# Half a gated block and VectorE's key tiles ahead of the key-value product and the sample updates; a new layout for the adaLN product

## The chip, the cores and the metric

The kernel runs on one core of a Trainium2 chip. Five engines work side by side, each with its own fixed list of instructions: TensorE (PE in the profile; its weight loads are PEld), VectorE (DVE), ScalarE (ACT), GpSimd (POOL) and SyncE (SP), whose queue here issues nearly all transfers. They wait for each other by semaphores. The metric is device time of one execution in microseconds; lower is better. The kernel before was timed in three runs: 1280.69, 1283.85 and 1285.78 us, median 1283.85.

## The reference, cut to what matters

One inference step of a trunk of two layers, for 512 prompt tokens and 8 sample tokens (520 in all), width 1024, four heads of 256. Each layer mixes an mLSTM branch and a causal convolution branch:

```python
mod = jax.nn.silu(c) @ w_ada + b_ada
shift, scale, gate = jnp.split(mod[:, None, :], 3, axis=-1)
h = rmsnorm(x, norm_w) * (1.0 + scale) + shift
proj = h @ w_in
xm, zm, ga, gb, zc, gm, gc = jnp.split(proj, N_SPLITS, axis=-1)
...
h, C, n, m = mlstm_chunkwise(q, k, v, i_pre, logf, C0, n0, m0)
hm = (hm + skip * xm_c) * jax.nn.silu(zm)
y_m = hm @ w_br_m
u = ga * jax.nn.sigmoid(gb)
u, cbuf = causal_dwconv(u, cbuf0, cconv_w, cconv_b)
u = jax.nn.silu(layernorm(u, cln_w, cln_b))
u = u * jax.nn.silu(zc)
y_c = u @ w_br_c
merged = jax.nn.sigmoid(gm) * y_m + jax.nn.sigmoid(gc) * y_c
x = x + gate * (merged @ w_out)
```

The chunkwise mLSTM amounts to this for the prompt: weights from gates and scores, `S = (q k^T) * exp(D)`; numerator `S v`; and a new memory `C = sum ws k v^T`, which is an output. For each sample token the old memory `C0` is scaled and a rank-one term is added: `C_new = a * C + ws * k v^T`, an output too.

## The kernel before, in words

**Dense products.** `dense` (L180) multiplies a 128-column weight with all tokens in two halves of 260, in three products of split numbers (high by high, high by low, low by high): 24 matmuls of 128x260 a half, 48 for an output block. `split_w` (L163) loads a raw weight on SP's queue, ACT casts it to the high part (whi, L173), POOL subtracts for the low part (wlo, L176).

**Order.** A scheduler orders the instructions of each engine before the run. It follows the program's order as priority, its own estimate of times, and `tc.issue_after(ins)`, which lets the instructions in its block be placed only behind `ins`. PSUM comes from pools: three buffers with tag "d" (dense products), three with tag "m", two with tag "cv".

**adaLN.** The modulation has six chunks of 512 columns a layer. Chunks 0 to 3 hold scale and shift; hh and hl, the high and low part of the normed input, need one for each two k. Chunks 4 and 5 hold the gate, which only `residual` (L321) reads, at the end of the layer. `ada_load` brings a chunk in four loads of 512 KB. `ada_mul` (L286) multiplies it: 8 matmuls of 32x512, one for each k, into the column group k % 4, so that the group sums stand in four sets of 32 rows; ACT copies 128x512 (asb, from the pool "t520" of four buffers). Its `tail` sums the four groups and turns them with four matmuls with a selection matrix (sel32), and VectorE adds the bias into mod. In the first layer chunks 0 to 3 run inside the first gated block (`dense_pair`, L237, the rows L248), whose k-th step needs the k-th hh. Chunks 4 and 5 follow that block. The second layer's chunks 0 and 1 are multiplied in the first layer's GM and GC stages, the others at the layer's change and just behind it.

**Stages of a layer.** gab 0 (first gated block of the convolution branch), xm with q, k, v, the gates, gab 2, then the heads (L924 to L941), normaliser and output of the mLSTM, ZM, GM (merge gate of the mLSTM, L1013 to L1026), GC, layer norm, ZC, BRC, OUT.

**Heads.** For head h: `values` turns v (ptok) and splits it into v1h and v1l; `scores` makes pu and pds and the weights dd and P; `sample` loads the memories of two sample tokens (cb) and multiplies them with q (pqc); `nxt`, the first part of a gated block left over from the head before; `apply` multiplies P with v (ppv); `keys` turns k (ptok) and scales it into a high part on ACT (kwh) and a low part on VectorE (kw); `updates` change cb (POOL scales, L777, and VectorE adds, L780) and write it out; `gab_b` (L527) runs the second part of the next gated block, 48 dense matmuls; `memory` is the key-value product (pcf) from kwh, kw and v. Before the first head, pst and pvt turn the gates and the samples' values.

Of the kernel before, what the change touches and what calls it, by code (L numbers as in the profile page):

```python
# [1 line left out]

# [1 line left out]

# [16 lines left out]
L = 2  # L21
# [8 lines left out]
H = 4  # L30
# [45 lines left out]
def build(nc, tc, ctx, ap):  # L76
# [60 lines left out]
    class Pairs:  # L137
# [7 lines left out]
        def tail(self, i, n):  # L145
            return self.tiles[i][:, :, T - n:T]

    def t520(name):
        return tmp.tile([128, T], F32, tag="t520", bufs=T5B, name=name)
# [127 lines left out]
    def ada_load(l, c, tag):  # L277
        raw = ada_tile(tag)
        for kp in range(0, 4, 2):
            ada_half(l, c, raw, kp)  # L280
        return raw

    def ada_chunk(l, adas, c, tag, ps=("m", 3)):
        return ada_mul(adas, c, ada_load(l, c, tag), ps)

    def ada_mul(adas, c, raw, ps=("m", 3), stream=False):  # L286
        vec, mod, sa = adas
        acc = pm("ada", *ps)
        for n in range(KT):
            k = n if stream else KT - 1 - n  # L290
            r = 32 * (k % 4)
            te.matmul(acc[r:r + 32, :], cT[:, k, :], raw[k // 2][:, k % 2, :], start=(n < 4), stop=(n >= 4))  # L292
        asb = t520("asb")
        s.copy(asb[:, 0:512], acc)

        def tail():
            pt = pm("adat", *ps)
            ks = slice(c * 4, c * 4 + 4)
            for i in range(4):
                te.matmul(pt[:, i * 9:i * 9 + 9], asb[:, i * 128:(i + 1) * 128], sel32[:, 0:9], start=True, stop=True)  # L300
            v.tensor_tensor(out=mod[:, ks, :], in0=pt[:, 0:36].rearrange("p (m r) -> p m r", r=9),
                            in1=vec[:, O_BADA + c * 4:O_BADA + c * 4 + 4].unsqueeze(2).to_broadcast([128, 4, 9]),
                            op=ALU.add)
            if c < 4:
                o = 2 * c
                v.scalar_tensor_tensor(out=sa[:, o:o + 2, :], in0=mod[:, 4 * c:4 * c + 2, :], scalar=1.0,
                                       in1=vec[:, O_NORM + o:O_NORM + o + 2].unsqueeze(2).to_broadcast([128, 2, 9]),
                                       op0=ALU.add, op1=ALU.mult)
        return tail
# [100 lines left out]
    for l in range(L):  # L410
# [113 lines left out]

            return [first, second] + [lambda sft=sft: tap(1 - sft % 2, sft) for sft in range(3, W31)] + [last]

        def gab_b(k, raw=False, w=None):  # L527
            wb, wa = w or split_w(ap["wst"][l, PR_GAB + k], 2)
            sg = t520("sg")

            def evb(c, p):
                if raw or w:
                    s.copy(sg[:, c], p)
                    if w and c is HALF[1]:
                        s.activation(sg, sg, AF.Sigmoid)
                else:
                    s.activation(sg[:, c], p, AF.Sigmoid)

            def eva(c, p):
                v.tensor_tensor(out=u[:, k, c], in0=p, in1=sg[:, c], op=ALU.mult)  # L540

            def gab_a():
                if w:
                    dense_pair(wb, wa, hh, hl, evb, eva, hook)
                    mm = None
                else:
                    mm = dense(wa, hh, hl, KT, eva)
                nc.sync.dma_start(ap["o_conv_p"][l, :, k], u[:, k, TP - W31 + 1:TP])
                conv31_sample(k)
                filler.extend(conv31_tasks(k))  # L550
                return mm

            if not w:
                dense(wb, hh, hl, KT, evb)
                if raw:
                    s.activation(sg, sg, AF.Sigmoid)
            return gab_a

        def gab(k, raw=False, w=None):
            return gab_b(k, raw, w)()  # L560

        mtail = sml.tile([128, KT, W4 - 1], F32, tag="mtail", name="mtail")

# [58 lines left out]
            return proj(tuple(a[:, 512:1024] for a in w), xcs, kk, h, DH ** -0.5)  # L622

        gab(0, w=w01)
        if l == 0:
            gtails = [ada_chunk(l, adas, 4, "q"), ada_chunk(l, adas, 5, "v")]
        else:
            gtails.append(ada_mul(adas, *raws.pop(0)))
        for tail in gtails:
            tail()  # L630
        xc = big.tile([128, KT, T], F32, tag="xc", name="xc")
        q = big.tile([128, KT, T], F32, tag="q", name="q")
        kk = Pairs("k", F32, "kk")
# [123 lines left out]
        def sample(b):  # L757
            cb = s8.tile([128, KT, V1], F32, tag="s8", bufs=S8B, name="cb")
            nc.sync.dma_start(cb, ap["C0"][l, b])
            vb = s8.tile([128, H, V1], F32, tag="s4", bufs=2, name="vb")  # L760
            nc.sync.dma_start(vb.rearrange("p h c -> p (h c)"),
                              vsc[b].rearrange("h c -> (h c)").partition_broadcast(128))
            p = pm("pqc")
            for j in range(2):
                for h in range(H):
                    k = 2 * h + j
                    o = (k * TS + b) * TS
                    te.matmul(p[32 * h:32 * h + 32, 0:V1], zq[:, o:o + 32], cb[:, k, :],  # L768
                              start=(j == 0), stop=(j == 1))
            if b == 0:  # L770
                v.tensor_copy(qc, p[:, 0:V1])
            else:
                v.tensor_tensor(out=qc, in0=qc, in1=p[:, 0:V1], op=ALU.add)

            def update():
                for h in range(H):
                    g.tensor_scalar(out=cb[:, 2 * h:2 * h + 2, :], in0=cb[:, 2 * h:2 * h + 2, :],  # L777
                                    scalar1=bc[:, 0, h, b:b + 1], scalar2=1.0, op0=ALU.mult, op1=ALU.mult)
                    for j in range(2):
                        v.scalar_tensor_tensor(out=cb[:, 2 * h + j, :], in0=vb[:, h, :], scalar=wsk[:, h, j, b:b + 1],  # L780
                                               in1=cb[:, 2 * h + j, :], op0=ALU.mult, op1=ALU.add)
                nc.sync.dma_start(ap["o_C_s"][l, b], cb)

            return update

# [33 lines left out]
        def tok_major(src, h, a):  # L819
            p = pm("ptok")  # L820
            for b in range(2):
                for j in range(2):
                    o = (b * 2 + j) * 128
                    t0 = (2 * a + b) * 128
                    te.transpose(p[:, o:o + 128], src[:, 2 * h + j, t0:t0 + 128], ident)  # L825
            return p

        def mul3(p, first, last, ah, al, bh, bl):
# [3 lines left out]
        def mlstm(h):  # L832
# [42 lines left out]
            def keys():  # L875
                st["kwl"] = []
                p = [tok_major(kk, h, a) for a in range(2)]
                kwh = big.tile([128, 4, DH], F32R, tag=f"k{h}", name="kwh")
                st["kwh"] = kwh
                for a in range(2):  # L880
                    kt = tmp.tile([128, 2, DH], F32R, tag="t520", bufs=T5B, name="kw")
                    for b in range(2):
                        i = 2 * a + b
                        pb = p[a][:, b * 256:(b + 1) * 256]
                        s.activation(kwh[:, i, :], pb, AF.Copy, scale=ws[:, i:i + 1])
                        v.scalar_tensor_tensor(out=kt[:, b, :], in0=pb, scalar=ws[:, i:i + 1],
                                               in1=kwh[:, i, :].bitcast(F32), op0=ALU.mult, op1=ALU.subtract)
                        st["kwl"].append(kt[:, b, :])

            def apply():  # L890
                Ph, Pl = st["P"]
# [33 lines left out]
        for h in range(H):  # L925
            values, scores, keys, apply, memory = mlstm(h)
            values()
            pl = scores()
            if h == 0:
                sample_factors()  # L930
            updates = [sample(2 * h + i) for i in range(2)]
            if nxt:
                nxt()
            apply()
            keys()
            with tc.issue_after(pl.ins):
                updates[0]()
            nxt = gab_b(h + 3, True)
            memory()
            updates[1]()  # L940
            fill(F_H)  # L941

        s1 = sml.tile([128, 1], F32, name="s1")
# [64 lines left out]

        mrg = Pairs("v", F32, "mrg")
        if l + 1 < L:  # L1010
            adas = ada_start(l + 1)
            raw = ada_load(l + 1, 0, "xc")
        for m in range(KT):  # L1013
            wg, wb = split_w(ap["wst"][l, PR_GMB + m], 2)
            sg = t520("sgm")
            dense(wg, hh, hl, KT, lambda c, p: s.activation(sg[:, c], p, AF.Sigmoid))

            def ev(c, p):
                i = v.tensor_tensor(out=mrg[:, m, c], in0=p, in1=sg[:, c], op=ALU.mult)
                with tc.issue_after(i.ins):  # L1020
                    fill(F_GM)

            mm = dense(wb, hmh, hml, KT, ev)
            if l + 1 < L and m == 3:
                with tc.issue_after(mm.ins):
                    tail = ada_mul(adas, 0, raw)  # L1026

        sgc = Pairs("k", F32, "sgc")
        if l + 1 < L:
# [171 lines left out]
```

## Time and profile before

| | before |
|---|---|
| median of three runs | 1283.85 us |
| the profiled execution | 1279.5 us |
| its span, first to last instruction | 1277.8 us |
| mean granted TensorE clock | 0.993 |
| VectorE busy | 843.3 us (66%) |
| ACT busy | 531.8 us (42%) |
| POOL busy | 682.4 us (53%) |

The profile is of one execution. Its span leaves out 1.7 us of its own time. All rows below are of that execution and count from the start of the span. A row of a timeline gives start, duration, engine, line, operation, output and input tiles, shape, count of records, and in brackets how long the engine was idle before it and what ended that. A group's row gives busy time, mean duration of one in ns, and idle time before. One fp32 matmul leaves two records; a matmul of split numbers leaves one.

### The profile page before, as it was taken

The page shows a single profiled execution, that of the slowest core. Times are in us where ns is not written, and L with a number is a line of the kernel's source. Part 1 is how long each engine was busy: PE and PEld are TensorE (multiplying, and loading weights), DVE is VectorE, ACT ScalarE, POOL GpSimd, SP SyncE. Part 2 cuts the span into 40 slices and gives each one's busy share as a digit, 9 for nine tenths or more (in the row PEclk, how much of TensorE's full clock was granted, in tenths as well). Part 3 has the DMA queues.
Part 4 walks back from the last instruction along what each step waited for, and adds up shares of the span by engine and source line. Part 5 has one row for each costly group of instructions (what it writes and reads, how often), then busy time and mean ns, then how long its engine had stood idle before and what let it go on. Part 6 is the DMA issues. An engine that isn't in the chain of part 4 may idle for free.

```text
span 1277.8 us, 25802 instructions
## 1 busy us (share of the span) xinstructions
PE 1226.5 (96%) x10244; PEld 1155.6 (90%) x10244; DVE 843.3 (66%) x1735; ACT 531.8 (42%) x955; POOL 682.4 (53%) x899
## 2 busy tenths in 40 slices
PE   6999999999999999999999999999999999999996
PEld 3699988889999999899979997888899999989996
DVE  6495576667977993544257748666788899735424
ACT  3466554443332223532236655445434222344342
POOL 2356545556654446565635664444485545467572
PEclk9999999999999999999999999999999999999998
DMA  9632346653342342243932324566422232223322
GB/s 361 232 95 78 115 159 246 218 183 124 100 166 83 99 149 84 75 149 108 336 136 85 101 82 137 205 211 241 164 88 97 86 99 85 84 83 123 127 83 67
DMA packets 59929, 177.14 MB, mean 139 GB/s; under 512 B 13409, under 2 KB 21665, under 8 KB 55713
## 3 DMA queue, kind: packets, MB, share of 16 engines
q1 hardware_dynamic: 56928, 167.08, 38.6%
q10 hardware_dynamic: 2880, 8.42, 1.8%
q8 instruction: 80, 1.31, 0.4%
q14 instruction: 41, 0.33, 0.1%
HBM read 149.77 MB, written 25.71 MB: 137 GB/s over the span
## 4 chain that ended last, share of the span: by engine, by line
PE 80%; DVE 10%; ACT 3%; DMA 3%; POOL 2%; issue 1%; SPq 1%; DVEq 0%; ACTq 0%; POOLq 0%
PE pd L188 66%; DVE cb L780 4%; PE pds L864 3%; PE pd L248 2%; DMA o_C_p<-cf 2%; POOL wlo L176 2%; PE ada L292 1%; ACT whi L173 1%; PE pqc L768 1%; PE pcf L830 1%; DVE cv L515 1%; PE ppv L830 1%; PE pg L664 1%; DMA wada<-w_ada 1%; PE ptok L825 1%
## 5 line engine op out<-in xcount | busy, mean ns | idle before, releaser
L176 POOL TENSOR_TENSOR wlo<-raw,whi 128x256 fp32r<-128x256 f32 x680 | 523.5, 802 | 523.5 <-ACT whi L173 518.8
L188 PE MATMUL pd<-hh,whi 128*128 128x260 f32 x1728 | 495.4, 287 | 6.9 <-ACT szc L1051 5.3
L188 PE MATMUL pd<-hl,whi 128*128 128x260 f32 x1728 | 491.2, 284 | 0.0
L188 PE MATMUL pd<-hh,wlo 128*128 128x260 f32 x1728 | 490.8, 284 | 0.0
L188 PEld LDWEIGHTS pd<-hh,whi 128*128 128x128 f32 x1728 | 326.6, 189 | 14.5 <-ACT szc L1051 5.8
L188 PEld LDWEIGHTS pd<-hl,whi 128*128 128x128 f32 x1728 | 327.0, 189 | 0.4 <-issue 0.2
L188 PEld LDWEIGHTS pd<-hh,wlo 128*128 128x128 f32 x1728 | 326.8, 189 | 0.3 <-POOL wlo L176 0.2
L173 ACT CAST whi<-raw 128x1024 fp32r<-128x1024 f32 (+1 forms) x174 | 179.1, 1030 | 329.8 <-PE pd L188 276.4
L515 DVE SCALAR_TENSOR_TENSOR cv<-u,vec,cv 128x509 f32<-128x509 f32 (+6 forms) x448 | 296.5, 729 | 0.1
L780 DVE SCALAR_TENSOR_TENSOR cb<-vb,wsk,cb 128x257 f32<-128x257 f32 x128 | 72.7, 616 | 4.0 <-POOL cb L777 4.0
L188 PE MATMUL pd<-hmh,whi 128*128 128x260 f32 x256 | 72.4, 283 | 0.0
L188 PE MATMUL pd<-hml,whi 128*128 128x260 f32 x256 | 72.4, 283 | 0.0
L188 PE MATMUL pd<-hmh,wlo 128*128 128x260 f32 x256 | 72.3, 283 | 0.0
L188 PE MATMUL pd<-zl,whi 128*128 128x260 f32 x256 | 72.0, 283 | 0.0
L188 PE MATMUL pd<-zh,wlo 128*128 128x260 f32 x256 | 72.0, 283 | 0.0
L188 PE MATMUL pd<-zh,whi 128*128 128x260 f32 x256 | 71.8, 283 | 0.0
L188 PE MATMUL pd<-ml,whi 128*128 128x260 f32 x224 | 63.3, 283 | 0.0
L188 PE MATMUL pd<-mh,whi 128*128 128x260 f32 x224 | 63.3, 283 | 0.0
L188 PE MATMUL pd<-mh,wlo 128*128 128x260 f32 x224 | 63.2, 283 | 0.0
L324 DVE SCALAR_TENSOR_TENSOR xr<-pd,mod,xo 128x260 f32<-128x260 f32 (+1 forms) x32 | 15.3, 484 | 61.7 <-PE pd L188 38.9
L777 POOL TENSOR_SCALAR cb<-cb,bc 128x514 f32<-128x514 f32 x64 | 51.5, 825 | 1.3 <-PE pqc L768 1.3
L188 PE MATMUL pd<-xcs,whi 128*128 128x260 f32 x256 | 47.9, 287 | 3.0 <-ACT vv L568 2.9
(306 smaller groups left out, 2251.3 us busy)
## 6 DMA issues: line engine op xcount, KB each, us to landing
raw<-wst SPq DMA_DIRECT2D x160, 512.0 KB, 3.8
wada<-w_ada SPq DMA_DIRECT2D x36, 512.0 KB, 8.1
cb<-C SPq DMA_DIRECT2D x16, 1028.0 KB, 6.5
o_C_s<-cb SPq DMA_DIRECT2D x16, 1028.0 KB, 5.4
vb<-vsc SPq DMA_DIRECT2D x16, 514.0 KB, 5.5
wada<-w_ada ACTq DMA_DIRECT2D x12, 512.0 KB, 5.8
raw<-wqkv SPq DMA_DIRECT2D x8, 512.0 KB, 3.5
x<-x SPq DMA_DIRECT2D x4, 520.0 KB, 7.0
```

What stands on the lines that cost most here:

```text
L173: s.copy(hi, sl)
L176: g.tensor_tensor(out=lo[:, cs], in0=sl[:, cs], in1=hi.bitcast(F32)[:, cs], op=ALU.subtract)
L188: mm = te.matmul(p[:, 0:HT], a[:, ws], b[:, k, HALF[c]], start=(n == 0), stop=(n == 3 * nk - 1))
L248: te.matmul(p[:, 0:HT], a[:, ws], b[:, k, HALF[c]], start=(k == 0 and i == 0), stop=(k == KT - 1 and i == 2))
L292: te.matmul(acc[r:r + 32, :], cT[:, k, :], raw[k // 2][:, k % 2, :], start=(n < 4), stop=(n >= 4))
L324: v.scalar_tensor_tensor(out=x[:, m, c.start:c.start + n], in0=p[:, 0:n], scalar=mod[:, 16 + m, 0:1], in1=xo[:, c.start:c.start + n], op0= ...
L515: v.scalar_tensor_tensor(out=acc[a][:, sft:TP], in0=u[:, k, 0:TP - sft], scalar=wcol(sft), in1=acc[a][:, sft:TP], op0=ALU.mult, op1=ALU.add)
L664: te.matmul(pgs[n][32 * j:32 * j + 32, 0:HT], vec[:, o:o + 32], (q, kk, vv)[t][:, k, c], start=(r == 0), stop=(r == 5))
L777: g.tensor_scalar(out=cb[:, 2 * h:2 * h + 2, :], in0=cb[:, 2 * h:2 * h + 2, :], scalar1=bc[:, 0, h, b:b + 1], scalar2=1.0, op0=ALU.mult, o ...
L780: v.scalar_tensor_tensor(out=cb[:, 2 * h + j, :], in0=vb[:, h, :], scalar=wsk[:, h, j, b:b + 1], in1=cb[:, 2 * h + j, :], op0=ALU.mult, op ...
L830: te.matmul(p, a, b, start=(first and n == 0), stop=(last and n == 2))
L864: te.matmul(p[:, 0:n], kk[:, 2 * h + j, t0:t0 + 128], q[:, 2 * h + j, t0:TP], start=(j == 0), stop=(j == 1))
```

## The change

It has three parts.

1. **Layout of the adaLN product.** `ada_mul` makes 32 matmuls of 32x128 for a chunk instead of 8 of 32x512: for each k, four, one for each 128 columns, each into a column group of its own. The result is then already summed over k, 128x128. ACT copies 128x128 into a buffer of its own (tag "asb", two buffers) and no longer into "t520". The tail is one transpose instead of four matmuls.
2. **Place of chunks 4 and 5 of the first layer.** They leave their place behind gab 0 and come in the first layer's GM stage, behind m = 1 and m = 3, with their tails; the second layer's chunk 0 moves from m = 3 to m = 5. All three are loaded into the tile "xc", one after the other.
3. **Heads.** `gab_b` runs its first half as before and its second half behind the last transpose of kk; `memory` may be placed only behind the last matmul of that second half. The updates of the first of the two sample tokens are cut in two: heads 0 and 1 behind the scores, heads 2 and 3 behind the last kw too. Those of the second come behind the last kw. In the program `keys` now stands behind the first of these.

```diff
         for n in range(KT):
             k = n if stream else KT - 1 - n
-            r = 32 * (k % 4)
-            te.matmul(acc[r:r + 32, :], cT[:, k, :], raw[k // 2][:, k % 2, :], start=(n < 4), stop=(n >= 4))
-        asb = t520("asb")
-        s.copy(asb[:, 0:512], acc)
+            for j in range(4):
+                mm = te.matmul(acc[32 * j:32 * j + 32, 0:128], cT[:, k, :],
+                               raw[k // 2][:, k % 2, j * 128:(j + 1) * 128], start=(n == 0), stop=(n == KT - 1))
+        asb = sml.tile([128, 128], F32, tag="asb", bufs=2, name="asb")
+        s.copy(asb, acc[:, 0:128])
...
-            for i in range(4):
-                te.matmul(pt[:, i * 9:i * 9 + 9], asb[:, i * 128:(i + 1) * 128], sel32[:, 0:9], start=True, stop=True)
+            te.transpose(pt[:, 0:128], asb, ident)
...
-                dense(wb, hh, hl, KT, evb)
+                dense(wb, hh, hl, KT, evb, (0,))
+                with tc.issue_after(behind.ins) if behind else nullcontext():
+                    mm = dense(wb, hh, hl, KT, evb, (1,))
...
-        if l == 0:
-            gtails = [ada_chunk(l, adas, 4, "q"), ada_chunk(l, adas, 5, "v")]
-        else:
+        if l:
             gtails.append(ada_mul(adas, *raws.pop(0)))
...
             apply()
-            keys()
             with tc.issue_after(pl.ins):
-                updates[0]()
-            nxt = gab_b(h + 3, True)
-            memory()
-            updates[1]()
+                updates[0](range(2))
+            turned, kw = keys()
+            with tc.issue_after(kw.ins), tc.issue_after(pl.ins):
+                updates[0](range(2, H))
+            nxt, mm = gab_b(h + 3, True, behind=turned)
+            with tc.issue_after(mm.ins):
+                memory()
+            with tc.issue_after(kw.ins):
+                updates[1](range(H))
...
         if l + 1 < L:
+            late = adas
             adas = ada_start(l + 1)
-            raw = ada_load(l + 1, 0, "xc")
+            turns = [(late, l, 4), (late, l, 5), (adas, l + 1, 0)]
+            raw = ada_load(*turns[0][1:], "xc")
...
             mm = dense(wb, hmh, hml, KT, ev)
-            if l + 1 < L and m == 3:
+            if l + 1 < L and m % 2 == 1 and turns:
+                who, _, c = turns.pop(0)
                 with tc.issue_after(mm.ins):
-                    tail = ada_mul(adas, 0, raw)
+                    tail = ada_mul(who, c, raw)
+                if turns:
+                    raw = ada_load(*turns[0][1:], "xc")
+                    tail()
```

The engines' lists show where this puts the work. At three places they stand as follows; a row gives the line, the operation, output and input tiles, the shape, and how often it stands there in a row.

PE, first head of the first layer, before: pst and pvt turn gates and samples, ptok turns v, the pd rows are dense matmuls, pu begins the scores.

```order
L188 MATMUL pd<-hh,whi 128x260
L710 MATMUL pst<-ident,sxt 128x128 x4
L719 MATMUL pvt<-ident,vv 32x128 x8
L825 MATMUL ptok<-ident,vv 128x128 x2
L727 MATMUL pvt<-ones,prod 32x2 x8
L825 MATMUL ptok<-ident,vv 128x128 x2
L188 MATMUL pd<-hl,whi 128x260
```

The same place of the changed kernel:

```order
L188 MATMUL pd<-hh,wlo 128x260
L711 MATMUL pst<-ident,sxt 128x128 x4
L720 MATMUL pvt<-ident,vv 32x128 x8
L827 MATMUL ptok<-ident,vv 128x128 x4
L728 MATMUL pvt<-ones,prod 32x2 x8
L827 MATMUL ptok<-ident,vv 128x128 x4
L862 MATMUL pu<-ur,selr 128x512
L864 MATMUL pu<-mneg,identr 128x128
L866 MATMUL pds<-q,kk 128x512 x2
```

Before, the last row shown is the first of 20 dense matmuls; then come ptok, one more dense matmul, pu, and 17 more ahead of pds: 38. Now none stands between pst and pds, and 99 instead of 109 stand ahead of pst since the gates' work. The 48 come later, 25 of them between the transposes of kk and the first pcf.

VectorE, first head of the first layer, from the samples' product on, before: cb are the updates, bst and mv the statistics of the head's output, kw the key tiles, u the gated block's evacuation.

```order
L780 SCALAR_TENSOR_TENSOR cb<-vb,wsk,cb 128x257 x4
L798 BN_AGGR mv<-bst 128x2
L780 SCALAR_TENSOR_TENSOR cb<-vb,wsk,cb 128x257 x2
L800 SCALAR_TENSOR_TENSOR dn<-q,en 128x4
L797 BN_STATS bst<-q 128x6
L780 SCALAR_TENSOR_TENSOR cb<-vb,wsk,cb 128x257 x2
L886 SCALAR_TENSOR_TENSOR kw<-ptok,wsl,kwh 128x256 x2
L797 BN_STATS bst<-q 128x6
L540 TENSOR_TENSOR u<-pd,sg 128x260
```

The changed kernel there:

```order
L802 SCALAR_TENSOR_TENSOR dn<-q,en 128x4
L800 BN_AGGR mv<-bst 128x2
L803 TENSOR_TENSOR dn<-dn,q 128x4
L889 SCALAR_TENSOR_TENSOR kw<-ptok,wsl,kwh 128x256 x4
L781 SCALAR_TENSOR_TENSOR cb<-vb,wsk,cb 128x257 x12
L841 MEMSET v1l 128x4x2
L851 MEMSET v1h 128x4x2
L540 TENSOR_TENSOR u<-pd,sg 128x260
L850 TENSOR_TENSOR v1l<-ptok,v1h 128x2x256 x2
```

Four of the sixteen updates stay ahead of the statistics; the four kw come next, and the other twelve updates stand in one row behind them, ahead of u and v1l.

PE at the start, the end of gab 0's k loop, before: ada is the adaLN product, adat its tail, the L248 rows are gab 0.

```order
L292 MATMUL ada<-wada,cT 32x512 x2
L300 MATMUL adat<-sel_83,asb 128x9 x4
L248 MATMUL pd<-hh,whi 128x260 x2
L292 MATMUL ada<-wada,cT 32x512
L248 MATMUL pd<-hl,whi 128x260
```

The changed kernel's last chunk there, whose next rows are gab 0's last third with dense matmuls of xm (L188) between:

```order
L248 MATMUL pd<-hh,wlo 128x260
L300 MATMUL adat<-ident,asb 128x128
L188 MATMUL pd<-hh,whi 128x260
L188 MATMUL pd<-hl,whi 128x260
L248 MATMUL pd<-hh,whi 128x260 x2
L188 MATMUL pd<-hh,wlo 128x260
L188 MATMUL pd<-hh,whi 128x260
```

Before, gab 0 had chunk 4's product between its last rows (the single ada row and seven more behind it). Now twenty dense matmuls of xm stand there.

More of the change, by code (lines that the diff above doesn't have):

```diff
@@ L1 @@
-from contextlib import ExitStack
+from contextlib import ExitStack, nullcontext
 import numpy as np
@@ L298, in tail @@
             ks = slice(c * 4, c * 4 + 4)
-            for i in range(4):
-                te.matmul(pt[:, i * 9:i * 9 + 9], asb[:, i * 128:(i + 1) * 128], sel32[:, 0:9], start=True, stop=True)
-            v.tensor_tensor(out=mod[:, ks, :], in0=pt[:, 0:36].rearrange("p (m r) -> p m r", r=9),
+            te.transpose(pt[:, 0:128], asb, ident)
+            v.tensor_tensor(out=mod[:, ks, :], in0=pt[:, 0:128].rearrange("p (m r) -> p m r", r=32)[:, :, 0:9],
                             in1=vec[:, O_BADA + c * 4:O_BADA + c * 4 + 4].unsqueeze(2).to_broadcast([128, 4, 9]),
@@ L525, in conv31_tasks, with gab_b @@
             return [first, second] + [lambda sft=sft: tap(1 - sft % 2, sft) for sft in range(3, W31)] + [last]
-        def gab_b(k, raw=False, w=None):
+        def gab_b(k, raw=False, w=None, behind=None):
             wb, wa = w or split_w(ap["wst"][l, PR_GAB + k], 2)
@@ L551, in gab_a @@
                 return mm
+            mm = None
             if not w:
-                dense(wb, hh, hl, KT, evb)
+                dense(wb, hh, hl, KT, evb, (0,))
+                with tc.issue_after(behind.ins) if behind else nullcontext():
+                    mm = dense(wb, hh, hl, KT, evb, (1,))
                 if raw:
                     s.activation(sg, sg, AF.Sigmoid)
-            return gab_a
+            return gab_a, mm
         def gab(k, raw=False, w=None):
-            return gab_b(k, raw, w)()
+            return gab_b(k, raw, w)[0]()
         mtail = sml.tile([128, KT, W4 - 1], F32, tag="mtail", name="mtail")
@@ L624, in build @@
         gab(0, w=w01)
-        if l == 0:
-            gtails = [ada_chunk(l, adas, 4, "q"), ada_chunk(l, adas, 5, "v")]
-        else:
+        if l:
             gtails.append(ada_mul(adas, *raws.pop(0)))
-        for tail in gtails:
-            tail()
+            for tail in gtails:
+                tail()
         xc = big.tile([128, KT, T], F32, tag="xc", name="xc")
@@ L773, in sample, with update @@
                 v.tensor_tensor(out=qc, in0=qc, in1=p[:, 0:V1], op=ALU.add)
-            def update():
-                for h in range(H):
+            def update(hs):
+                for h in hs:
                     g.tensor_scalar(out=cb[:, 2 * h:2 * h + 2, :], in0=cb[:, 2 * h:2 * h + 2, :],
@@ L781, in update @@
                                                in1=cb[:, 2 * h + j, :], op0=ALU.mult, op1=ALU.add)
-                nc.sync.dma_start(ap["o_C_s"][l, b], cb)
+                if H - 1 in hs:
+                    nc.sync.dma_start(ap["o_C_s"][l, b], cb)
             return update
@@ L824, in tok_major @@
                     t0 = (2 * a + b) * 128
-                    te.transpose(p[:, o:o + 128], src[:, 2 * h + j, t0:t0 + 128], ident)
+                    tok_major.last = te.transpose(p[:, o:o + 128], src[:, 2 * h + j, t0:t0 + 128], ident)
             return p
@@ L877, in keys @@
                 p = [tok_major(kk, h, a) for a in range(2)]
+                turned = tok_major.last
                 kwh = big.tile([128, 4, DH], F32R, tag=f"k{h}", name="kwh")
@@ L885, in keys @@
                         s.activation(kwh[:, i, :], pb, AF.Copy, scale=ws[:, i:i + 1])
-                        v.scalar_tensor_tensor(out=kt[:, b, :], in0=pb, scalar=ws[:, i:i + 1],
-                                               in1=kwh[:, i, :].bitcast(F32), op0=ALU.mult, op1=ALU.subtract)
+                        last = v.scalar_tensor_tensor(out=kt[:, b, :], in0=pb, scalar=ws[:, i:i + 1],
+                                                      in1=kwh[:, i, :].bitcast(F32), op0=ALU.mult, op1=ALU.subtract)
                         st["kwl"].append(kt[:, b, :])
+                return turned, last
             def apply():
@@ L1023, in build @@
             mm = dense(wb, hmh, hml, KT, ev)
-            if l + 1 < L and m == 3:
+            if l + 1 < L and m % 2 == 1 and turns:
+                who, _, c = turns.pop(0)
                 with tc.issue_after(mm.ins):
-                    tail = ada_mul(adas, 0, raw)
+                    tail = ada_mul(who, c, raw)
+                if turns:
+                    raw = ada_load(*turns[0][1:], "xc")
+                    tail()
         sgc = Pairs("k", F32, "sgc")
```

## The prediction

> **What bounds the kernel now.** I read the page first: the busy time of each engine and the chain of work that ended last.
>
> ```profile
> PE 1226.5 (96%) x10244; PEld 1155.6 (90%) x10244; DVE 843.3 (66%) x1735; ACT 531.8 (42%) x955; POOL 682.4 (53%) x899
> PE 80%; DVE 10%; ACT 3%; DMA 3%; POOL 2%; issue 1%; SPq 1%; DVEq 0%; ACTq 0%; POOLq 0%
> ```
>
> TensorE (PE) is busy for 1226.5 of 1277.8 us and holds 80% of the chain. So an edit pays only if it takes work from PE, or ends a stretch in which PE waits. The second view lists what PE waited for, by releaser: total us, times, longest.
>
> ```profile
> PE pst L710 <- DVE sxt L688: 5.9, 2, 3.0
> PE pcf L830 <- ACT kwh L885: 4.5, 8, 0.6
> PE pcf L830 <- DVE kw L886: 3.1, 6, 0.6
> PE pd L248 <- ACT hh L433: 1.3, 1, 1.3
> PE ada L292 <- DMA wada<-w_ada: 1.2, 2, 1.0
> ```
>
> The two pcf rows (key-value product) add up to 7.6 us over the eight heads; pst (one 3.0 us wait at the first head of each layer) is 5.9. The last row matters because the start, below, partly hangs on landings.
>
> **Start: the adaLN chunks.** The timeline of PE, with the DMA queue's issues (SPq) and the landing times of the chunk weights, shows this. Columns: start, duration, engine, line, operation, tiles, count.
>
> ```profile
> 15.90 1.05 PE L292 MATMUL ada<-wada,cT 128*32 128x512 f32 x4 [0.24 <-DMA wada<-w_ada]
> 16.88 1.16 PE L203 MATMUL rb<-yi,ident 128*128 128x130 f32 x8
> 19.82 1.05 PE L292 MATMUL ada<-wada,cT 128*32 128x512 f32 x4 [0.98 <-DMA wada<-w_ada]
> 43.71 1.06 PE L300 MATMUL adat<-sel,asb 128*128 128x9 f32 x8 [0.69 <-ACT asb L294]
> 45.25 1.52 ACT L433 ACTIVATE hh<-x,mod,sa 128x512 fp32r<-128x512 f32 x2 [1.59 <-DVE sa L306]
> 46.12 0.51 PE L248 MATMUL pd<-hh,whi 128*128 128x260 f32 x2 [1.35 <-ACT hh L433]
> 48.45 1.92 PE L292 MATMUL ada<-wada,cT 128*32 128x512 f32 x14
> 52.30 0.28 PE L188 MATMUL pd<-hh,whi 128*128 128x260 f32 x1
> 52.42 0.28 PE L188 MATMUL pd<-hl,whi 128*128 128x260 f32 x1
> 57.53 1.92 PE L292 MATMUL ada<-wada,cT 128*32 128x512 f32 x16
> 59.38 1.06 PE L300 MATMUL adat<-sel,asb 128*128 128x9 f32 x8
> 60.29 0.37 PE L188 MATMUL pd<-hl,whi 128*128 128x260 f32 x1
> L292 PE MATMUL ada<-wada,cT 128*32 128x512 f32 x96 | 19.7, 629 | 1.2 <-DMA wada<-w_ada 1.2
> L300 PE MATMUL adat<-sel,asb 128*128 128x9 f32 x48 | 6.1, 254 | 0.7 <-ACT asb L294 0.7
> 10.64 13.19 SPq L275 DMA_DIRECT2D wada<-w_ada  x12
> DMA to landing us min/median/max: 8.1/9.0/10.7
> L195 PE MATMUL lnm<-u,ones 128*32 128x130 f32 x128 | 4.4, 277 | 0.0
> L768 PE MATMUL pqc<-cb,zq 128*32 128x257 f32 x256 | 15.6, 383 | 0.0
> ```
>
> One dense matmul takes 0.12 us (52.30 to 52.42). The two group rows are those of the window from 10 to 63.5 us: the first layer's six chunks cost PE 19.7 + 6.1 = 25.8 us, 4.3 each. A chunk without a break costs 1.85 (57.53 to 59.38) and its tail 0.91 (59.38 to 60.29). The rest is breaks: a lone pair of k costs 0.98 (15.90 to 16.88), over twice its quarter of 1.85, since its two matmuls stand in two of the four column groups and nothing runs beside the last pass.
>
> The trace has no instruction of the new form (32-column weights, N = 128, four column groups for each k). Its nearest row is the column sum lnm: 128 records, N = 130, four groups, 4.4 us, so 34 ns a record. Eight matmuls of old leave 16 records, so 32 leave 64: 64 x 34 ns = 2.2 us as an upper end. A floor is 1.85, the same columns as before. I take 1.95. A pair alone should now cost a quarter, 0.5. The tail falls from four matmuls (0.91) to one transpose; I take 0.15, between one matmul's pitch of 0.12 and a quarter of 0.91.
>
> If PE bound the whole start, four chunks at 1.95 + 0.15 would be 8.4, and 25.8 - 8.4 = 17.4 us would go, an upper end. But landings come up. The last of the twelve loads is issued at 10.64 + 13.19 = 23.8 and lands some 9.0 to 10.7 later, by 34.5 at the latest. From there: half a us for the last pair, 0.6 for the copy, 0.15 for the tail, then what lay between the old tail's start and the end of the two hh (43.71 to 46.77 = 3.06, less the 0.9 of the old tail, so some 2.2). hh of the last two k stands at about 38 to 39.5; before it was 46.8. Behind it are 24 matmuls of gab 0 and, by the order, 20 of xm between them: 44 x 0.12 = 5.3, with 0.8 for pieces that still wait, so about 45.4 where 52.30 stood, with 20 x 0.12 = 2.4 already done: **-9.3**. Of this 1.85 + 0.5 is chunk 4's product, which only moves. Chunk 5's product and the tails of 4 and 5 behind it go too: 1.85 + 2 x 0.91 = **-3.6**. The lower end, if landings kept the rest as it is, is 2.3 + 3.6 = 5.9 for both.
>
> **Chunks 4 and 5 come back** at m = 1 and 3 of the first layer's GM stage, where PE never waits: 2 x (1.95 + 0.15) = 4.2, with two breaks of the dense stream at 0.1: **+4.4**. Eight more loads of 512 KB go through SP's queue there. Each chunk's four are issued two columns of GM ahead of their use (2 x 96 dense matmuls, 23 us against at most 10.7 for a landing), so PE shouldn't wait; where a load holds up SP, the weights of the next column stand behind it, and they too are asked for a column ahead.
>
> **Second layer.** Two tails while the first layer runs, 0.8 to 0.15 each with a little lost at the break: **-1.2**. At the layer's change:
>
> ```profile
> 649.50 3.62 PE L292 MATMUL ada<-wada,cT 128*32 128x512 f32 x32
> 652.94 0.41 PE L195 MATMUL rmsn<-sqo,ones 128*32 128x130 f32 x8
> 653.27 1.95 PE L300 MATMUL adat<-sel,asb 128*128 128x9 f32 x16
> 657.46 1.13 PE L203 MATMUL rb<-yi,ident 128*128 128x130 f32 x8 [0.38 <-DVE yi L160]
> ```
>
> rb waits for a chain through DVE that starts at rmsn of 652.94. Its two tails (1.95) go, yet most of that turns into a longer wait for yi. What is won: rmsn now stands behind one chunk and a half (2.9 us instead of 3.44), -0.55, and two later tails, -1.35: **-1.9**.
>
> **Heads: the pcf waits.** Before, the product starts right after the transposes of kk, and its first and third operand are still being scaled (7.6 us in the rows above). Now 25 dense matmuls (half of a gated block; 3.0 us) stand ahead of it, against waits of 0.6; kw leads on DVE. **-7.6**, the bounds 0 and 7.6.
>
> **Heads: what the half block covered.** Layer 0, head 0, from PE's timeline and the windows (busy, granted clock, DMA share):
>
> ```profile
> 177.96 1.04 PE L710 MATMUL pst<-ident,sxt 128*128 128x128 f32 x4 [2.98 <-DVE sxt L688]
> 185.06 1.29 DVE L848 TENSOR_TENSOR v1l<-ptok,v1h 128x512 fp32r<-128x512 f32 x2 [0.52 <-ACT v1h L847]
> 186.75 1.88 PE L864 MATMUL pds<-q,kk 128*128 128x512 f32 x4
> 194.88 0.39 PE L830 MATMUL ppv<-v1h,Ph 128*128 128x258 f32 x1
> 178.00:181.40 3.40, 3.40 (x41) 0.50 0.14 41
> ```
>
> pst waits for a chain on DVE that no edit shortens, so it starts where it did; the order has 10 dense matmuls fewer ahead of it, and none of the 38 that stood between pst and pds. These 48 (5.8 us) are done later instead. The stretch shrinks by less: the chain pst, v1h, v1l, dd is DVE's and ACT's, and its fillers held pds back to 186.75 with its first dd ready some 3 us earlier, so ppv comes forward by about 3.1. Cost 5.8 - 3.1 = 2.7 a layer: **+5.4**. Bounds: 0 (all fillers were in the way) to 5.8 + 1.7 = 7.5 a layer, where 1.7 is a second window at half clock (3.4 us at 0.50).
>
> The row of 178.00 shows that clock behind a wait of only 2.98. [...]
>
> Heads 1 to 3 of each layer keep dense matmuls at these places, but DVE now runs twelve cb updates in one row, between kw and v1l:
>
> ```profile
> L780 DVE SCALAR_TENSOR_TENSOR cb<-vb,wsk,cb 128x257 f32<-128x257 f32 x128 | 72.7, 616 | 4.0 <-POOL cb L777 4.0
> 224.74 1.76 DVE L780 SCALAR_TENSOR_TENSOR cb<-vb,wsk,cb 128x257 f32<-128x257 f32 x2 [0.59 <-POOL cb L777]
> 231.42 1.66 DVE L780 SCALAR_TENSOR_TENSOR cb<-vb,wsk,cb 128x257 f32<-128x257 f32 x4
> 224.00 6.43 POOL L777 TENSOR_SCALAR cb<-cb,bc 128x514 f32<-128x514 f32 x8
> 227.08 1.03 PE L825 MATMUL ptok<-ident,kk 128*128 128x128 f32 x8
> 245.75 0.59 PE L864 MATMUL pds<-q,kk 128*128 128x512 f32 x1
> ```
>
> An update takes 0.88 us beside POOL's scaling (224.74) and 0.42 once that has ended (231.42). kk is turned from 227.08 on, in 1.0 us; four steps of kwh at 0.56 (the pcf wait) and a last kw of some 0.5 end at 230.8, when POOL has ended (224.00 + 6.43 = 230.4). Twelve updates at the mean of 0.62 take 7.4, to 238.2; then u and v1l, some 1.7: 239.9. The next head's pds stood at 245.75; by the order 75 dense matmuls lie between kk's transposes and it instead of 96 (-2.5), and the pcf waits (-1.0) are gone: 242.2. So I cost this at nothing, with 2.3 us of cover.
>
> **Sum**: -9.3 - 3.6 + 4.4 - 1.2 - 1.9 - 7.6 + 5.4 = -13.8 against the profiled run's own 1279.5 (span 1277.8). That run lies 4.4 below the median of the three, 1283.85. The change is laid on the median: 1270.
>
> **Rivals.**
> 1. Uncovered first head: both layers pay the upper bound, +15 instead of +5.4, so -4.2: 1279.7. For it: half clock follows the wait already. Against: most of a longer wait would itself use up the slow window.
> 2. Start bound by landings: 5.9 instead of 12.9, so -6.8: 1277. For it: the waits for wada. Against: the waits for wada before the last tail are the two shown, 1.2 us in all; the rest of the start was PE's own work.
> 3. The pcf wait only changes its releaser (u, cb or kw late), so the -7.6 fails: 1277.7.
> 4. Slower: the row of twelve updates stays under contention. v1l is late from (242.2 - 1.7 - 230.8) / 12 = 0.81 us an update. From 1.06 the wait reaches 3 us, which at head 0 brought a half-clock window worth 1.7; then the six later heads pay 4.7 each: 28 - 13.8 = +14, 1298. The largest row is 0.88, so this needs more than the trace has shown.
> 5. Slower too: the new products cost by the instruction. [...] No run here shows such a cost. In rows: if each of the 64 records takes what one of pqc does (15.6 us / 256 = 61 ns, though twice as wide), a chunk costs 3.9, and twelve chunks 23 more: +9, 1293. lnm's 34 ns speaks against it.
>
> **How the numbers follow.** Forecast 0.58; rivals 0.14, 0.12, 0.08, 0.04 and 0.04. The forecast's own range is 1264 to 1276; with rivals 1 to 3 the range is 1263 to 1281. A measurement of this kernel tells about 0.5% (6.4 us) from no change, so faster is below 1277.4: the forecast, and half of rivals 2 and 3 and some of 1, 0.74; same 0.19; slower 0.07.
>
> **What would show it.** Right: the first xm matmul after gab 0 near 45 to 46 us; ada groups of about 2 us; no pcf rows among PE's waits; pst still about 3 to 4 us, and pds of head 0 some 3 us nearer to it. Wrong: waits of L248 for wada or whi before 45 us; waits of pds, ppv or pu for DVE v1l, u or ACT dd in the later heads; clock of 0.5 in more than one window at a head; 3 us or more for an ada group.

## The result, and the profile after

| | before | changed |
|---|---|---|
| median of six runs each | 1283.57 us | 1274.09 us |
| lowest to highest | 1280.69 to 1286.39 | 1271.62 to 1278.29 |
| ratio, 95% interval | | 0.9929 (0.9905 to 0.9952) |
| the profiled execution | 1279.5 us | 1278.3 us |
| its span | 1277.8 us | 1276.5 us |
| mean granted TensorE clock | 0.993 | 0.976 |

The change makes the kernel 9.5 us faster, 0.7%. The forecast was 13.8 faster; 1274.09 lies inside its range of 1263 to 1281. Mind the profiles: the changed kernel's profiled execution is the slowest of its six runs, and the one before lies below all six of its own. They differ by 1.2 us only, so their difference shows where time went, and not how much in the median.

The page of the changed kernel, its busy row, and then what PE waited for:

```profile
PE 1219.3 (96%) x10736; PEld 1168.1 (92%) x10736; DVE 860.7 (67%) x1735; ACT 528.6 (41%) x955; POOL 683.3 (54%) x899
...
PE pst L711 <- DVE sxt L689: 8.3, 2, 4.1
...
PE pths L969 <- DVE xc L925: 6.9, 2, 3.5
PE pd L188 <- ACT xms L587: 5.2, 8, 1.8
PE ada L292 <- DMA wada<-w_ada: 4.6, 3, 3.3
...
PE pqc L769 <- DMA cb<-C: 1.5, 1, 1.5
PE pds L866 <- DVE v1l L850: 1.3, 2, 0.7
```

Both pcf rows (7.6 us before) are gone. In their place: pst waits 2.4 longer; pths, two transposes at the end of the heads that waited for nothing, waits 6.9; the start waits 3.4 more for chunk weights; the dense matmuls that read xms (xm, split) wait 2.4 more (2.8 in all before); pqc and pds have small waits that are new. The lower clock is the second half of the story. Windows (start and end, length, PE busy, clock, DMA share, GB/s) of the changed kernel at the start, at head 0 of layer 0, and behind the heads:

```profile
19.60:27.20 7.60, 6.52 (x78) 0.55 1.03 415
165.80:180.20 14.40, 11.61 (x57) 0.53 0.44 134
166.40:180.10 13.70, 11.51 (x57) 0.50 0.45 140
180.20:185.20 5.00, 5.00 (x54) 1.00 0.40 146
306.00:313.70 7.70, 6.38 (x31) 0.56 0.50 154
```

Before, the half clock of head 0 lasted 3.4 us. Now it lasts 13.7 (166.40 to 180.10), and new stretches stand at the start and behind the heads, each behind one of the new waits. Summed up to 1275 us of the span, a clock below full took 7.5 us of full-speed time before and 30.3 in this execution (length times one minus the clock, in windows of 0.85 us).

### The profile page after: what moved, and what is told of

It reads as the page before. It is cut to its first block, busy times and chain, and to the rows that moved or that the text cites. A ratio compares the mean times of both kernels' runs of the same rounds, so it can differ in the third digit from the quotient of the medians.

```text
span 1276.5 us, 26752 instructions
## 1 busy us (share of the span) xinstructions
PE 1219.3 (96%) x10736; PEld 1168.1 (92%) x10736; DVE 860.7 (67%) x1735; ACT 528.6 (41%) x955; POOL 683.3 (54%) x899
## 4 chain that ended last, share of the span: by engine, by line
PE 83%; DVE 7%; ACT 4%; DMA 3%; issue 1%; POOL 1%; SPq 0%; DVEq 0%; ACTq 0%
PE pd L188 68%; PE pds L866 3%; PE ppv L832 2%; PE pd L248 2%; PE pcf L832 2%; ACT whi L173 1%; PE ada L292 1%; PE pqc L769 1%; DVE upr L492 1%; PE ptok L827 1%; DMA cb<-C 1%; PE pg L665 1%; DMA wada<-w_ada 1%; DVE cb L781 1%; POOL wlo L176 1%
## 5 line engine op out<-in xcount | busy, mean ns | idle before, releaser
L176 POOL TENSOR_TENSOR wlo<-raw,whi 128x256 fp32r<-128x256 f32 x680 | 528.9, 809 | 503.9 <-ACT whi L173 487.4
L188 PE MATMUL pd<-hh,whi 128*128 128x260 f32 x1728 | 496.6, 287 | 3.8 <-ACT szc L1065 3.8
L188 PE MATMUL pd<-hh,wlo 128*128 128x260 f32 x1728 | 493.4, 286 | 0.0
L188 PE MATMUL pd<-hl,whi 128*128 128x260 f32 x1728 | 493.3, 286 | 0.0
L188 PEld LDWEIGHTS pd<-hh,whi 128*128 128x128 f32 x1728 | 328.2, 190 | 7.6 <-ACT szc L1065 4.4
L188 PEld LDWEIGHTS pd<-hh,wlo 128*128 128x128 f32 x1728 | 328.7, 190 | 1.0 <-issue 0.6
L188 PEld LDWEIGHTS pd<-hl,whi 128*128 128x128 f32 x1728 | 328.2, 190 | 1.1 <-issue 0.2
L781 DVE SCALAR_TENSOR_TENSOR cb<-vb,wsk,cb 128x257 f32<-128x257 f32 x128 | 80.0, 694 | 0.5 <-POOL cb L778 0.5
L188 PE MATMUL pd<-hmh,whi 128*128 128x260 f32 x256 | 72.4, 283 | 0.0
L188 PE MATMUL pd<-hml,whi 128*128 128x260 f32 x256 | 72.4, 283 | 0.0
L188 PE MATMUL pd<-hmh,wlo 128*128 128x260 f32 x256 | 72.4, 283 | 0.0
L188 PE MATMUL pd<-zl,whi 128*128 128x260 f32 x256 | 71.9, 283 | 0.0
L188 PE MATMUL pd<-zh,wlo 128*128 128x260 f32 x256 | 71.9, 283 | 0.0
L188 PE MATMUL pd<-zh,whi 128*128 128x260 f32 x256 | 71.7, 283 | 0.0
L188 PE MATMUL pd<-ml,whi 128*128 128x260 f32 x224 | 63.2, 283 | 0.0
L188 PE MATMUL pd<-mh,whi 128*128 128x260 f32 x224 | 63.2, 283 | 0.0
L188 PE MATMUL pd<-mh,wlo 128*128 128x260 f32 x224 | 63.2, 282 | 0.0
L188 PE MATMUL pd<-xcs,whi 128*128 128x260 f32 x256 | 48.2, 288 | 2.2 <-ACT vv L571 2.0
L778 POOL TENSOR_SCALAR cb<-cb,bc 128x514 f32<-128x514 f32 x64 | 48.7, 782 | 1.3 <-PE pqc L769 1.3
```

Of the source, the lines that this page charges most:

```text
L176: g.tensor_tensor(out=lo[:, cs], in0=sl[:, cs], in1=hi.bitcast(F32)[:, cs], op=ALU.subtract)
L188: mm = te.matmul(p[:, 0:HT], a[:, ws], b[:, k, HALF[c]], start=(n == 0), stop=(n == 3 * nk - 1))
```

## The experiments

Three parts, so first each alone. The edits are parts of the diff above, on the kernel before.

**Layout alone.** Part 1 of the change, nothing else.

> Kernel before with the new adaLN layout alone (32 matmuls of 128 columns and one transpose a chunk; chunks 4 and 5 stay behind gab 0, heads as before). Theory A (the start is PE's own work, so the layout pays there and at the later tails): the first layer's start loses breaks and tails, 7 to 9 us, the other chunks' tails 3, so 1273 to 1276 beside 1283.6, ratio about 0.992. Theory B (the start is bound by landings, only tails pay): 3 to 4 us, ratio 0.997. Theory C (cost by the instruction): slower.

Measured: 1277.0 us beside 1283.83, ratio 0.9946 (0.9927 to 0.9965), so 6.8 us: between theories A and B, nearer to A. Theory C is out.

**Layout and place.** Parts 1 and 2.

> Kernel before with the new layout and with chunks 4 and 5 in the GM stage; heads as before. Theory A (the stages of the changed profile add up: -10.4 up to the gates, +4 in GM, -3 at later tails): 9 us faster, ratio 0.993, as much as the whole change brings. Theory B (the move costs in GM what it saves at the start): the same as the layout alone.

Measured: 1272.98 us, ratio 0.9919 (0.9902 to 0.9936), 10.9 us. Theory A. These two parts bring all that the whole change brings.

**Heads alone.** Part 3.

> Kernel before with the change in the heads alone. Theory A (the changed profile's stages: pcf waits gone, -7.6, but the first head of each layer 5 to 6 us later and a new wait of pths of 3.5 us a layer, with half clock behind both): 0 to 6 us slower. Theory B (the sum on record, -7.6 + 5.4): 2 us faster. Theory C (the head part carries the gain): 5 us or more faster.

Measured: 1283.59 us, ratio 1.0004 (0.9988 to 1.0019): no difference. That is theory A's lower end; C is out, and B's 2 us (0.9984) lie just beyond the interval. So seven us of waits go, and as much comes back.

Where it comes back is read in the traces by milestones: when the first matmul of the gates (pg), of ppv of head 0 and 3, and of the layer norm's sum (lnm) starts in a trace. The table gives the change of each stretch against before, in us, with 0.12 put in for every dense matmul that was moved past the milestone. The last three columns belong to runs further down: the whole change with pths freed, and with one half of the head part each.

| stretch | changed | layout, place | pths freed | key tiles alone | half block alone |
|---|---|---|---|---|---|
| start to pg | -10.4 | -11.9 | -11.8 | -10.7 | -12.4 |
| layer 0: pg to ppv of head 0 | +6.4 | +0.7 | +6.4 | +1.2 | +6.2 |
| ppv of head 0 to head 3 | -4.6 | +2.0 | -5.2 | -2.3 | +2.4 |
| ppv of head 3 to lnm (GM with it) | +7.0 | +4.2 | +1.3 | +2.7 | +9.8 |
| layer 1: pg to ppv of head 0 | +5.4 | +0.7 | +5.2 | +0.6 | +5.6 |
| ppv of head 0 to head 3 | -6.6 | +0.5 | -6.4 | -2.9 | +2.2 |
| ppv of head 3 to lnm | +2.1 | -0.3 | -4.3 | -1.6 | +4.7 |

Two suspects in the changed column: head 0 (+6.4 and +5.4) and the end of the heads (pths). The next runs take them one at a time.

**Head 0 covered.** In head 0 nothing is held back:

```diff
-            nxt, mm = gab_b(h + 3, True, behind=turned)
-            with tc.issue_after(mm.ins):
+            nxt, mm = gab_b(h + 3, True, behind=turned if h else None)
+            with tc.issue_after(mm.ins) if h else nullcontext():
                 memory()
```

> Changed kernel, but in head 0 of each layer the half block isn't held back and the key-value product doesn't wait for it, so that PE's order there is that of before: 38 dense matmuls between pst and pds again. Theory A (the lost cover and the half clock behind it cost 5 us a layer): pst to ppv free of half clock beyond one window, pcf waits of head 0 back (1.1 a layer), in all 7 to 9 us faster than the changed kernel, ratio to before 0.986 to 0.988. Theory B (only work was moved): within 2 us of the changed kernel, ratio 0.992 to 0.994.

Measured: 1272.65 us, ratio 0.9928 (0.991 to 0.9946): theory A fails, the time is that of the changed kernel. Head 0 is covered again (its stretch falls from +6.4 to +1.7), but the cover is only taken from head 1: there 48 dense matmuls fewer stand ahead of ppv now (the stretch from head 0 to head 3 goes from -4.6 to -0.3), and new waits come up:

```profile
PE pths L969 <- DVE xc L925: 6.3, 2, 3.5
PE pst L711 <- DVE sxt L689: 5.9, 2, 3.0
PE pqc L769 <- DMA cb<-C: 4.7, 3, 2.4
...
PE ppv L832 <- DVE qc L774: 3.0, 2, 1.8
```

**What pths waits for.** VectorE's and POOL's timelines of the changed kernel around it, then PE's:

```profile
299.95 6.02 DVE L492 TENSOR_TENSOR upr<-us,vec 128x248 f32<-128x248 f32 x1
306.01 0.59 DVE L493 TENSOR_REDUCE u<-upr 128x8 f32<-128x248 f32 x1
306.52 0.74 DVE L925 SCALAR_TENSOR_TENSOR xc<-pth,vec,xc 128x512 f32<-128x512 f32 x1
299.64 0.56 POOL L815 TENSOR_SCALAR q<-q,scl 128x256 f32<-128x256 f32 x1
300.16 5.55 POOL L176 TENSOR_TENSOR wlo<-raw,whi 128x256 fp32r<-128x256 f32 x8
307.32 0.69 PE L969 MATMUL pths<-ident,nt 128*128 128x128 f32 x2 [3.54 <-DVE xc L925]
```

pths needs a PSUM buffer that xc empties, and xc stands behind upr. upr, a product of 128x248, takes 6.02 us, where the median of its sixteen is 0.41; it ends 0.27 us after POOL's row of eight wlo without a gap. Two runs: one changes upr's form, one takes pths out of the queue.

```diff
-            v.tensor_tensor(out=pr, in0=us, in1=cw.unsqueeze(2).to_broadcast([128, W31, TS]), op=ALU.mult)
+            v.scalar_tensor_tensor(out=pr, in0=us, scalar=1.0, in1=cw.unsqueeze(2).to_broadcast([128, W31, TS]),
+                                   op0=ALU.mult, op1=ALU.mult)
```

> Changed kernel; the one product upr of the sample convolution (128x248) is written as a scalar_tensor_tensor with scalar 1 instead of a tensor_tensor, the order of every engine else as in the changed kernel. Theory A (VectorE's tensor_tensor with two SBUF inputs is held for as long as POOL runs its row of eight wlo, 5.5 us, and a scalar_tensor_tensor only shares, as the cb updates do at 0.88): upr at the end of the heads takes under 2 us instead of 6.02, the wait of pths (6.9) falls under 3, and 5 to 9 us go: 1265 to 1269. Theory B (any two-input operation is held by POOL): upr stays at some 6 us, time as the changed kernel, 1274.

Measured: 1274.93 us, ratio 0.9938 (0.9918 to 0.9958); upr's longest is 6.04. Theory B: the form isn't it.

```diff
-        pt = pm("pths")
+        pt = pm("pths", "d")
```

> Changed kernel with the two transposes pths in a PSUM buffer of tag d instead of m, so that they don't wait for VectorE to empty pth. Theory A (the wait of pths, 6.9 us, and the half clock behind it are lost time that nothing gives back): the waits go, 7 to 10 us faster than the changed kernel, 1264 to 1267. Theory B (VectorE is the bound there; upr's 6 us only move to the next matmul that needs pth's buffers or xc): a new wait of 3 us a layer on pth or on the ZM stage, time within 2 us of the changed kernel.

Measured: 1265.09 us, ratio 0.9865 (0.9842 to 0.9889), 9.0 below the changed kernel's median: theory A. upr is still held, 5.60 us here, but no one on PE waits for it:

```profile
297.59 5.60 DVE L492 TENSOR_TENSOR upr<-us,vec 128x248 f32<-128x248 f32 x1
303.12 0.28 DVE L972 TENSOR_TENSOR hsm<-pths,vec 128x32 f32<-128x32 f32 x2
303.32 0.62 DVE L493 TENSOR_REDUCE u<-upr 128x8 f32<-128x248 f32 x1
```

So the wait of 6.9 with the half clock behind it was pure loss of 8 to 9 us (by the ratios and by the medians), on PE alone. Both edits together, and with upr's other form:

> Changed kernel with head 0 ordered as before and pths in the other buffer. Theory A (the two new losses are independent): 1272.7 of head 0 covered, less 7 to 9, so 1264 to 1266, ratio 0.985 to 0.987, faster than all so far. Theory B (the loss at pths only moves): 1272.

Measured: 1266.63 us, ratio 0.9876 (0.9854 to 0.9897): no better than pths alone, as head 0's cover brought nothing before.

> The kernel of the run before this, with upr as a scalar_tensor_tensor too. Theory A (VectorE is held by POOL): no upr above 2 us, 0 to 3 us more than the run before this, 1262 to 1266. Theory B: no difference.

Measured: 1265.86 us, ratio 0.9868 (0.9844 to 0.9893), upr 6.07: theory B, no difference.

**The head part, split.** It has two halves: kw ahead of the updates, and half a gated block ahead of pcf. Each alone, with parts 1 and 2 and with pths freed. First kw's place; `gab_b` and `memory` stand as before:

```diff
-            nxt, mm = gab_b(h + 3, True, behind=turned)
-            with tc.issue_after(mm.ins):
-                memory()
+            nxt, mm = gab_b(h + 3, True)
+            memory()
```

> Changed kernel with pths in the other buffer, and of the head part only the place of kw and the updates: no half of the gated block is held back, pcf doesn't wait for it. Theory A (the half block takes away at head 0 what it brings at pcf, so that kw's place carries the heads' gain): kw's waits (3.1) gone, kwh's (4.5) stay, cover at head 0 back, time within 2 us of the kernel with both (1265.1). Theory B (the half block carries it): near layout and place alone, 1271 to 1273.

Measured: 1264.39 us beside 1282.75, ratio 0.9855 (0.9834 to 0.9875). Theory A: as good as both halves. pcf's waits for kwh stay, kw's shrink (theory A had said that they go), head 0 keeps its cover:

```profile
PE pst L711 <- DVE sxt L689: 5.9, 2, 3.0
...
PE pcf L832 <- ACT kwh L888: 4.5, 8, 0.6
...
PE pcf L832 <- DVE kw L889: 1.7, 8, 0.2
```

The 1.4 us by which kw's waits shrink are the smaller part of the gain over layout and place alone. That kernel's pds also waits for ACT's dd, and this wait is gone here:

```profile
PE pds L862 <- ACT dd L865: 2.8, 3, 1.1
```

At head 1 of the first layer 17, 3 and 12 dense matmuls now stand between the later rows of pu and pds, where with layout and place alone one and two stand. pths waits for nothing with layout and place alone, so freeing it should add nothing there; no run shows that by itself.

Then the half block, with the updates as they stood before:

```diff
-            with tc.issue_after(pl.ins):
-                updates[0](range(2))
             turned, kw = keys()
-            with tc.issue_after(kw.ins), tc.issue_after(pl.ins):
-                updates[0](range(2, H))
+            with tc.issue_after(pl.ins):
+                updates[0](range(H))
...
-            with tc.issue_after(kw.ins):
-                updates[1](range(H))
+            updates[1](range(H))
```

> Changed kernel with pths in the other buffer, and of the head part only the half block ahead of pcf; the updates stand as before, ahead of kw. Theory A: pcf's waits for kwh gone, head 0 uncovered with half clock (5 to 6 us a layer), no better than layout and place alone, 1271 to 1275. Theory B (the half block carries the gain): 1265 to 1267.

Measured: 1296.68 us, ratio 1.0085 (1.0052 to 1.0118): slower than before, which neither theory said. Its eight runs lie far apart, from 1282.52 to 1299.92. PE's waits:

```profile
PE pcf L832 <- DVE kw L889: 14.1, 8, 2.2
PE pst L711 <- DVE sxt L689: 8.3, 2, 4.2
...
PE pth L923 <- DVE xc L925: 6.8, 2, 3.5
```

With the dense matmuls run ahead of pcf, and kw still behind the updates on VectorE, pcf has nothing left to stand behind: it waits 14.1 us for kw. pth waits 6.8 more, and the trace has four windows of half clock that the one with pths freed doesn't have. The half block pays only if kw comes early, and then kw's place alone gives the same time.

**A shorter chain at head 0.** The transposes pst and what follows them are moved in the program behind the values of head 0, so that pvt, the transposes of v, v1h and v1l come ahead of pst:

```diff
-        pt = pm("pst")
...
             values()
+            if h == 0:
+                pt = pm("pst")
...
             pl = scores()
```

> Kernel with pths in the other buffer (1265.1), with head 0's values (transposes of v, v1h, v1l) and the samples' pvt ahead of pst instead of behind, so that PE has work in the wait for sxt and the chain to pds is shorter. Theory A (the uncovered chain and its half clock cost 5 to 6 us a layer): pst's wait falls from 4.2 towards 2, one or two half-clock windows fewer, 4 to 8 us faster, 1257 to 1261. Theory B (VectorE's chain alone sets pds): within 2 us.

Measured: 1261.95 us, ratio 0.9844 (0.9824 to 0.9864), beside 0.9865 for the kernel it starts from. The intervals overlap, so 2 to 3 us are likely and not certain, below theory A's 4 to 8. pst's wait didn't fall (8.5 in all, now for v1l): its first clause fails. What fell is the half clock at head 0: 10.2 and 6.8 us in the two layers, where the kernel with pths freed has 13.7 in each.

> The kernel with the key tiles' part alone, with head 0's values ahead of pst too, where dense work of the whole gated block stands between pst, pu and pds. Theory A: pst's wait under 1.5 us and no half clock at head 0, 3 to 7 us faster than the key tiles alone, fastest of all, 1257 to 1262. Theory B: within 2 us of the key tiles alone.

Measured: 1261.6 us, ratio 0.9838 (0.9817 to 0.9859), the fastest of all, beside 0.9855 for the key tiles alone: likely faster, not certain. The time is in theory A's range, but pst still waits 2.9 and some half clock is left. Windows of this kernel at head 0:

```profile
167.90:171.70 3.80, 3.80 (x32) 0.55 0.67 195
171.70:183.20 11.50, 11.50 (x92) 1.00 0.63 210
```

The half clock lasts 3.4 us (3.80 x 0.45 / 0.50), one window, in each layer. The key tiles alone have 6.8 there, the changed kernel 13.7. Between pst and pds stand 23 dense matmuls here, 38 with the key tiles alone and none in the changed kernel.

## Why the prediction was right, point by point

The forecast, faster by about 1%, holds in its sign, and its range holds the time. The terms:

- **Start, -12.9.** Up to pg the traces show -10.4 (changed) and -11.9 (layout and place). The mechanism was right: groups of the new product in the second layer's chunks show its price.

```profile
L292 PE MATMUL ada<-wada,cT 128*32 128x128 f32 x256 | 7.8, 273 | 0.0
```

  Four chunks in 7.8 us are 1.95 each, the value taken. What is missing is a longer wait for the second chunk's weights and the half clock behind it:

```profile
20.68 1.08 PE L292 MATMUL ada<-wada,cT 128*32 128x128 f32 x16 [3.35 <-DMA wada<-w_ada]
```

  This wait was 0.98. The first chunk got done sooner, and its successor's landing didn't: a piece of rival 2, worth 1 to 2.5 us.
- **Chunks 4 and 5 in GM, +4.4.** Between head 3 and lnm, the kernel with layout and place shows +4.2.
- **Second layer, -1.2 and -1.9.** From rmsn to rb it is -1.1 in every trace with the new layout, where -0.55 was said. Not in the sum: the wait of szc in the first layer (2.67 before, 0.39 now) and the half clock behind it went, with 37 more dense matmuls ahead of the layer norm's second sum; and a half-clock window worth 1.7 us came up in the second layer near 695, behind two waits for xms, of 1.08 and 1.75 us; before had only one of that size, of 1.76. Together, parts 1 and 2 were forecast at -11.6 and measured -10.9.
- **pcf waits, -7.6.** Gone, all of them, as said; the stretch from head 0 to head 3 got 4.6 and 6.6 us shorter in the two layers, more than the waits between these milestones (3.1 in the first layer). The rest lies in the pitch, from start to next start without these waits: in the first layer pcf's matmuls take 8.6 us there instead of 9.7, pu's 3.8 instead of 5.2, ptok's 4.5 instead of 5.2. The sum had no term for that.
- **Head 0, +5.4: the step that failed in size.** It said 2.7 a layer, with at most one more half-clock window in the upper bound of 7.5. Measured: 6.4 and 5.4. The 48 matmuls (5.8) were moved as said, and pst to pds got 2.5 us shorter (8.8 to 6.3). But pds and what follows ran at half clock (its first row took 3.78 us instead of 1.88), so that pst to ppv took 17.6 us instead of 16.9: the 3.1 that was to come back didn't. This was rival 1's mechanism, at some four fifths of its price (11.8 of 15). A sign of being wrong that stands on record, half clock in more than one window at a head, came.
- **pths, 9 us: the step that was missing.** The sum followed the heads up to the last pcf and gave the stretch behind them no term. There VectorE's list and POOL's meet in another phase, upr is held, and a transpose on PE stands behind it. No row of before shows it: upr's longest there is 1.14.

So the heads' -2.2 came out as -0.2 alone and as +1.4 on top of the other parts (10.9 against 9.5, within what the intervals leave open); and without the new wait the head part brings about 7.7 us (18.6 against 10.9, each beside its own before), more than forecast. That the total lies in the range is owed to parts 1 and 2. Within the head part, more gain from head 0 to head 3 (11.2 us where 7.6 were forecast) and more loss at head 0 (11.8 for 5.4) offset each other in part, which was luck.

At head 0 of the changed kernel half clock lasts from 166.4 to 180.1, four times the 3.4 us that it lasted before. Counted back from its end in steps of 3.4, the windows begin at 176.7, 173.3, 169.8 and 166.4. A wait ends in each of the first three: for sxt at 167.59 (1.19 us of its wait at half clock, which is what was said against rival 1), for stT at 171.41 (0.34 us), for v1l at 173.92 (0.65 us). Only in the last window is PE busy throughout (3.40 of 3.40 us), and at its end the clock is back. The second layer's four windows show the same (PE idle for 1.73, 0.35, 0.64 and 0 us). From these two stretches the author estimates that a small wait can cost a whole window more; no run took the wait for stT or v1l away by itself. The upper bound on record allowed for one window more, taken from the single one before, and three came; its 7.5 us weren't passed all the same (6.4 and 5.4), as pst to pds got 2.5 us shorter. With the key tiles alone PE is busy for 5.97 of 6.75 us around pst (166.45 to 173.20), and two windows pass; in the fastest kernel it is busy throughout (the window rows above), and the clock is back after one, 3.4 us.

## What to carry to other kernels

Dense work moved ahead of one wait is taken from the cover of another: list all the waits that it covered, as half clock behind the uncovered ones can cost more than the waits (at head 0, over both layers, the waits of pst, ptok and pds grew by 4.4 us, and the half clock from 3.4 to 13.7 us a layer, worth 10.3 us in all). Where two edits meet on one wait, run each alone: here one of them gave the whole gain and the other alone was slower than before. A small operation on an engine that is off the path can hold a PSUM buffer that TensorE's next instruction needs (upr, 6.02 us here); give that instruction a buffer of another queue (9.0 us here).

## What was not expected of the hardware

- VectorE's upr was held at the end of the heads in eight of the traces (the changed kernel and seven variants), in both layers: the longest of each trace takes 5.5 to 6.1 us, where the medians are 0.41 to 0.57. In the changed kernel both take 6.02; each began 0.31 to 0.32 us after one of POOL's operations had begun and ended 0.27 us after a gapless row of eight wlo on POOL. A tensor_tensor (6.02) and a scalar_tensor_tensor (6.04) are held alike. In the fastest kernel upr's longest is 0.99. Other VectorE operations run on beside such rows (26 cb updates of the changed kernel, 0.98 at most), so what decides who is held stays open. That POOL's row is the cause is argued from the times; no run took the row away.
- Executions of one kernel spread by 6.7 us (changed) with no edit, against a measured effect of 9.5. A half-clock window can hang on little: nine traces with the new layout have half clock near 695, in the changed kernel behind PE's waits for xms of 1.08 and 1.75 us; two, the fastest kernel's among them, have none, though PE's longest wait for xms is 1.8 us in all eleven. Why is open.
